# The last product of a gated MLP kernel: its second half of tokens first, to a bank of its own, combined and stored beside the first half

## The chip, the cores and the metric

One core of one Trainium2 chip. The metric is the device time of one execution in microseconds (us), of several executions, and beside it the span and the trace of one profiled execution.

## The reference

```python
# x: (8, 1024, 1024), w_gate and w_up: (1024, 4096), w_down: (4096, 1024), all float32
gate = x @ w_gate
up = x @ w_up
gate = 0.5 * gate * (1 + np.tanh(np.sqrt(2 / np.pi) * (gate + 0.044715 * gate ** 3)))
h = gate * up
return (h @ w_down).astype(np.float32)
```

## The kernel before

The 8192 tokens go through in eight passes of 1024. Each pass makes h for its tokens and multiplies it by w_down. From the fourth pass on both steps use a fast matrix scheme: fewer block products, more additions. The second step of such a pass is a list of 26 products of blocks. Their results are gathered in PSUM banks ("chains") and added by VectorE with signs into fp32 tiles; each of the 16 tiles is stored when it is complete. The list ends like this:

```python
DOWN = [
    # ... (cut)
    ('mul', 22, 'h5', 6, False),        # product into chain 6
    ('acc', 11, 11, 1, 1, -1, 1), ('acc', 5, 5, 1, -1, 1, -1), ('x',), ('x',),
    ('mul', 23, 'h1', 4, False),        # the last product, into chain 4
    ('acc', 5, 5, 6, -1, 1, 5), ('acc', 7, 7, 6, 1, -1, 9), ('x',), ('acc', 8, 8, 4, 1, 1, 2),
]
```

Only `('acc', 8, 8, 4, ...)` needs the last product; the two before it read chain 6. A product is 32 matmuls, two halves of tokens (m) in turn at each of 16 steps (j), both halves in one bank of 512 columns:

```python
def product(e, js):
    _, entry, h, c, first = e
    lhs, rhs = place[h], q_chunk(entry)
    for j in js:
        for m in range(2):
            nc.tensor.matmul(
                ps_all[:, bank[c], m * MQ : (m + 1) * MQ],     # MQ = 256
                lhs[:, j, m * P : (m + 1) * P],
                rhs[:, j, :],
                start=(first and j == 0 and m == 0),
                stop=(j == NP - 1),
                skip_group_check=True,
            )

def store(tile, o):
    q, c = divmod(o, 4)
    r0 = p * TOK + q * MQ
    nc.sync.dma_start(
        out=out2[r0 : r0 + MQ, c * MQ : (c + 1) * MQ].rearrange("(m p) c -> p m c", p=P),
        in_=tmp[:, t[tile]].rearrange("p (m c) -> p m c", m=2),
    )

# for an 'acc':
    nc.vector.scalar_tensor_tensor(
        tmp[:, t[v]], ps_all[:, bank[c]], float(sc * OSC), tmp[:, t[w]],
        MUL, ADD if st > 0 else SUB,
    )
# ... (cut: a store is put on a list and issued after the next product, or at the end)
```

## Time and profile before

| | us |
|---|---|
| time, median of 3 runs | 2256.03 (2255.78 to 2256.38) |
| span of the profiled execution | 2253.6 |
| TensorE busy | 2245.6 |
| last matmul ends | 2249.31 |
| last store lands (its last semaphore update) | 2.88 later |
| last instruction ends | 1.42 after that |

How to read it: nearly the whole span is one row of matmuls. What this change can touch is the tail, from the end of the last matmul to the end of the span, 4.30 us. I split it at the landing of the last store, because before the landing it is work (combine, issue, movement of the data, and the stretch from the last data to the landing, 0.35 us here) and after it only the engines' closing steps. That last stretch before the landing I call the confirmation. The ends, landings and closing steps are timestamps of the trace, which has them to a nanosecond; the page's views round to 0.01 or 0.1 us.

### The profile page before, as it was taken

What the parts mean: (1) busy time and instruction counts of PE and PEld (TensorE: products, weight loads), DVE (VectorE), ACT (ScalarE), POOL (GpSimd) and SP (SyncE); (2) the same over time, 40 slices, a digit from 0 to 9 for tenths busy, and PEclk for the clock granted to TensorE, in tenths of its full rate; (3) what the DMA queues carried; (4) which work ended last, traced back from release to release, by engine and by line L of the source; (5) the groups of instructions that cost most, each with busy time, mean ns of one, the idle gap of its engine ahead of it and who ended that gap; (6) DMA issues with size and microseconds to landing.
All of it is one profiled execution on the core that took longest, in us unless ns stands there. A gap on an engine that the chain in (4) does not pass through costs nothing.

```text
span 2253.6 us, 42764 instructions
## 1 busy us (share of the span) xinstructions
PE 2245.6 (100%) x16616; PEld 1624.2 (72%) x16616; DVE 1565.1 (69%) x2187; ACT 955.4 (42%) x1863; POOL 674.6 (30%) x825
## 2 busy tenths in 40 slices
PE   9999999999999999999999999999999999999999
PEld 4444444444444445888888888888888888888888
DVE  6666458883588755877776677666786667866674
ACT  4443135651365622666125550356404653055520
POOL 1332013330133300555014540255403543044520
PEclk9999999999999999999999999999999999999999
DMA  9898969999999999999998999988998889998886
GB/s 243 164 210 215 289 180 243 258 270 291 243 229 249 281 304 352 332 343 366 302 337 276 320 309 310 324 267 328 314 322 314 283 310 317 322 309 276 285 292 225
DMA packets 309117, 642.46 MB, mean 285 GB/s; under 512 B 79088, under 2 KB 185328, under 8 KB 288368
## 3 DMA queue, kind: packets, MB, share of 16 engines
q1 hardware_dynamic: 254128, 566.57, 73.5%
q0 software_dynamic: 54784, 73.14, 19.5%
q8 instruction: 130, 2.13, 0.4%
q14 instruction: 75, 0.61, 0.1%
HBM read 574.36 MB, written 138.41 MB: 316 GB/s over the span
## 4 chain that ended last, share of the span: by engine, by line
PE 87%; DMA 2%; SPq 1%; DVE 0%; issue 0%; DVEq 0%
PE ps L857 40%; PE ps L1108 20%; PE ps L635 17%; PE ps L1000 10%; DMA wd_quads<-x_sums 1%; SPq L255 0%; DMA ring<-wd_ops 0%; DVE x_sums L278 0%; DVE h_a L932 0%; DVE tmp L1177 0%; SPq L496 0%; DVEq L278 0%; SPq L544 0%
## 5 line engine op out<-in xcount | busy, mean ns | idle before, releaser
L857 PEld LDWEIGHTS <-ring 128*128 128x128 f16 x8320 | 814.1, 98 | 94.4
L834 POOL TENSOR_TENSOR h_a<-tmp 128x256 f16<-128x256 f32 x640 | 468.0, 750 | 840.6 <-ACT tmp L822 833.5
L857 PE MATMUL ps<-x_sums,ring 128*128 128x256 f16 x5760 | 655.8, 273 | 0.0
L819 DVE TENSOR_TENSOR tmp<-tmp,ps 128x512 f32<-128x512 f32 x640 | 414.3, 683 | 147.1 <-PE ps L857 90.2
L635 PEld LDWEIGHTS <-ring 128*128 128x128 f16 x2632 | 257.4, 98 | 311.2 <-DVE ring L360 0.9
L804 ACT COPY tmp<-ps 128x512 f32<-128x512 f32 x520 | 304.2, 585 | 237.0 <-PE ps L857 163.3
L635 PE MATMUL ps<-x_sums,ring 128*128 128x512 f16 x1504 | 340.1, 379 | 0.2 <-DVE ring L360 0.2
L822 ACT ACTIVATE tmp<-tmp 128x256 f32<-128x256 f32 x640 | 263.7, 418 | 173.2 <-DVE tmp L817 79.5
L857 PE MATMUL ps<-x_b,ring 128*128 128x256 f16 x2560 | 305.6, 273 | 0.0
L817 DVE TENSOR_TENSOR tmp<-ps,tmp 128x512 f32<-128x512 f32 x240 | 165.4, 689 | 145.2 <-ACT tmp L804 99.8
L635 PE MATMUL ps<-x_b,ring 128*128 128x512 f16 x1128 | 259.1, 379 | 0.0
L661 POOL TENSOR_TENSOR h_a<-tmp 128x512 f16<-128x512 f32 x94 | 141.1, 1501 | 377.4 <-ACT tmp L659 265.3
L1108 PEld LDWEIGHTS <-h_a 128*128 128x128 f16 x2240 | 219.2, 98 | 25.3
L1000 PE MATMUL ps<-ring,h_a 128*128 128x512 f16 x1024 | 222.3, 379 | 0.6 <-DMA ring<-wd_ops 0.6
L1108 PE MATMUL ps<-ring,h_a 128*128 128x256 f16 x1920 | 216.1, 273 | 0.0
L1000 PEld LDWEIGHTS <-h_a 128*128 128x128 f16 x1152 | 112.6, 98 | 136.8 <-DMA ring<-wd_ops 1.1
L654 DVE TENSOR_TENSOR tmp<-ps,tmp 128x512 f32<-128x512 f32 x188 | 127.3, 685 | 108.0 <-ACT tmp L646 106.5
L1165 ACT ACTIVATE tmp<-ps 128x512 f32<-128x512 f32 x60 | 35.3, 597 | 362.6 <-PE ps L1108 274.6
L1177 DVE SCALAR_TENSOR_TENSOR tmp<-ps,tmp 128x512 f32<-128x512 f32 x120 | 81.1, 690 | 97.5 <-PE ps L1108 66.7
L360 DVE TENSOR_TENSOR ring<-ring 128x1024 f16<-128x1024 f16 x188 | 139.7, 757 | 11.7 <-DMA ring<-in_w_up_dram 7.5
L646 ACT COPY tmp<-ps 128x512 f32<-128x512 f32 x188 | 109.8, 586 | 77.8 <-PE ps L635 77.8
L1108 PE MATMUL ps<-ring,x_sums 128*128 128x256 f16 x1120 | 126.3, 273 | 0.0
(102 smaller groups left out, 1534.0 us busy)
## 6 DMA issues: line engine op xcount, KB each, us to landing
ring<-w_ops SPq DMA_DIRECT2D x480, 512.0 KB, 4.9
ring<-wd_quads SPq DMA_DIRECT2D x110, 1024.0 KB, 6.9
ring<-wd_ops SPq DMA_DIRECT2D x35, 1024.0 KB, 8.2
out_dram<-tmp SPq DMA_DIRECT2D x128, 256.0 KB, 6.6
w_ops<-h_s SPq DMA_DIRECT2D x128, 256.0 KB, 6.8
ring<-in_w_gate_dram POOLq DMA_DIRECT2D x23, 1024.0 KB, 10.6
ring<-in_w_up_dram POOLq DMA_DIRECT2D x23, 1024.0 KB, 17.9
wd_quads<-x_sums SPq DMA_DIRECT2D x131, 128.0 KB, 6.5
```

The costliest lines, as they stand in the source:

```text
L360: nc.vector.tensor_tensor(o, a, b, op)
L635: nc.tensor.matmul(ps(b, w), lhs[:, k], rhs[:, k, :], start=(first and k == 0), stop=(k == KH - 1), skip_group_check=True,)
L654: nc.vector.tensor_tensor(o, ps("b", w), o, ADD)
L661: nc.gpsimd.tensor_tensor(hq[TO[n]][:, i, :], tmp[:, t[n, 1]], tmp[:, t[n, 0]], MUL)
L804: nc.scalar.copy(tmp[:, t[o[1]]], ps_all[:, bank[o[2]]])
L817: nc.vector.tensor_tensor(d, b, a, SUB)
L819: nc.vector.tensor_tensor(d, a, b, ADD if o[4] == "add" else SUB)
L822: nc.scalar.activation(d, d, GELU, scale=GSC)
L834: nc.gpsimd.tensor_tensor(h, tmp[:, t[o[1]], MQ : 2 * MQ], g, MUL)
L857: nc.tensor.matmul(ps_all[:, bank[c], w * MQ : (w + 1) * MQ], lhs[:, w, k], rhs[:, k], start=(first and w == 0 and k == 0), stop=(k == KH ...
L1000: nc.tensor.matmul(ps_all[:, bank[b, g]], lhs[:, j, g * P : (g + 1) * P], dc[:, n, :], start=(first and j == 0), stop=(j == NP - 1), skip_ ...
L1108: nc.tensor.matmul(ps_all[:, bank[c], m * MQ : (m + 1) * MQ], lhs[:, j, m * P : (m + 1) * P], rhs[:, j, :], start=(first and j == 0 and m ...
```

## The change

Intent: let the part of the work that has to wait for the very last matmul be half as large. The second half of the tokens is multiplied first, into a free bank; while TensorE then works on the first half, VectorE combines the second half and its store goes out. Only a combine of 256 columns and a store of 128 KB are left behind the last matmul. The core of the diff:

```diff
+        def last_product(e, events):
+            _, entry, h, c, _ = e
+            (fin,) = [f for f in events if f[0] == "acc" and f[3] == c]
+            # ... (cut)
+            other = ps_free.popleft()
+            d, (b0, b1) = tmp[:, t[v]], (slice(0, MQ), slice(MQ, 2 * MQ))
+
+            def part(m, b):
+                for j in range(NP):
+                    nc.tensor.matmul(
+                        ps_all[:, b, m * MQ : (m + 1) * MQ],
+                        place[h][:, j, m * P : (m + 1) * P],
+                        q_chunk(entry)[:, j, :],
+                        start=(m == 1 and j == 0),
+                        # ... (cut)
+                    )
+
+            def sum_up(b, s, op):
+                nc.vector.scalar_tensor_tensor(
+                    d[:, s], ps_all[:, b, s], float(sc * OSC), d[:, s], MUL, op
+                )
+
+            def send(m):
+                nc.sync.dma_start(
+                    out=out2[r0 + m * P : r0 + (m + 1) * P, o % 4 * MQ : (o % 4 + 1) * MQ],
+                    in_=d[:, m * MQ : (m + 1) * MQ],
+                )
+
+            part(1, other)
+            sum_up(bank[c], b1, ADD if st > 0 else SUB)
+            # ... (cut: stores that are due, the combines of chain 6, their stores)
+            part(0, bank[c])
+            sum_up(other, b1, ADD)
+            send(1)
+            sum_up(bank[c], b0, ADD if st > 0 else SUB)
+            send(0)
 # ... (cut)
+            if e[0] == "mul" and p == NPASS - 1 and i == end:
+                last_product(e, DOWN[i + 1 :])
+                break
```

More of the change, by code (lines that the diff above doesn't have):

```diff
@@ L1115, in product @@
                     )
+        def last_product(e, events):
+            _, entry, h, c, _ = e
+            (fin,) = [f for f in events if f[0] == "acc" and f[3] == c]
+            _, v, w, _, sc, st, o = fin
+            assert v == w and o >= 0 and not [f for f in events if f[0] == "snap"]
+            other = ps_free.popleft()
+            d, (b0, b1) = tmp[:, t[v]], (slice(0, MQ), slice(MQ, 2 * MQ))
+            r0 = p * TOK + o // 4 * MQ
+            def part(m, b):
[5 more added lines that the diff above has]
+                        start=(m == 1 and j == 0),
+                        stop=(j == NP - 1),
+                        skip_group_check=True,
+                    )
[10 more added lines that the diff above has]
+            sum_up(bank[c], b1, ADD if st > 0 else SUB)
+            for f in todo:
+                f()
+            todo.clear()
+            for f in events:
+                if f[0] == "acc" and f is not fin:
+                    acc(f)
+            for f in todo:
+                f()
+            todo.clear()
+            part(0, bank[c])
[3 more added lines that the diff above has]
+            send(0)
@@ new lines, in acc, with last @@
+        def acc(e):
+            _, v, w, c, sc, st, o = e
+            if v not in t:
+                t[v] = tmp_free.popleft()
+            nc.vector.scalar_tensor_tensor(
+                tmp[:, t[v]], ps_all[:, bank[c]], float(sc * OSC), tmp[:, t[w]],
+                MUL, ADD if st > 0 else SUB,
+            )
+            if v != w:
+                used(w, DOWN.index(e))
+            if o >= 0:
+                def last(v=v, o=o):
+                    store(v, o)
+                    tmp_free.append(t.pop(v))
+                todo.append(last)
+            if last_chain[c] == DOWN.index(e):
+                ps_free.append(bank[c])
@@ L1139, in down_fast @@
         count = 0
+        end = max(i for i, e in enumerate(DOWN) if e[0] == "mul")
         for i, e in enumerate(DOWN):
+            if e[0] == "mul" and p == NPASS - 1 and i == end:
+                last_product(e, DOWN[i + 1 :])
+                break
             if e[0] == "mul":
@@ L1173, in down_fast @@
             elif e[0] == "acc":
-                _, v, w, c, sc, st, o = e
-                if v not in t:
-                    t[v] = tmp_free.popleft()
-                nc.vector.scalar_tensor_tensor(
-                    tmp[:, t[v]], ps_all[:, bank[c]], float(sc * OSC), tmp[:, t[w]],
-                    MUL, ADD if st > 0 else SUB,
-                )
-                if v != w:
-                    used(w, i)
-                if o >= 0:
-                    def last(v=v, o=o):
-                        store(v, o)
-                        tmp_free.append(t.pop(v))
-                    todo.append(last)
-                if last_chain[c] == i:
-                    ps_free.append(bank[c])
+                acc(e)
             elif work:
```

## The prediction

> **What bounds the kernel now.** I read the page's busy shares first, then the slices, then the chain that ended last, and only then the last 10 us. The busy shares:
>
> ```profile
> span 2253.6 us, 42764 instructions
> ...
> PE 2245.6 (100%) x16616; PEld 1624.2 (72%) x16616; DVE 1565.1 (69%) x2187; ACT 955.4 (42%) x1863; POOL 674.6 (30%) x825
> ```
>
> TensorE is busy for the whole span but for 8.0 us; no other engine is near. The slices show full granted clock throughout. The change leaves the number and kind of matmuls as they are, so it can win only in those 8 us, and of them only in the part at the end. The chain of waits in order of time shows how little that is (start, length, what):
>
> ```profile
> 1976.84 181.65 PE ps L857 x1664
> 2158.49 90.84 PE ps L1108 x832
> 2249.33 0.02 issue
> 2249.35 0.69 DVE tmp L1177
> ```
>
> From 279 us on the chain is TensorE alone: the five last passes are blocks of 181.65 to 181.69 and of 90.83 or 90.84 us, so repeatable to 0.04 us. 90.84/832 = 109.2 ns from matmul to matmul, and 181.65/1664 = 109.2 ns in the block before. Behind the last matmul hangs one VectorE instruction. The timeline of the last 8 us (start, length, engine, line, what, idle before it and its releaser):
>
> ```profile
> 2245.33 3.98 PE L1108 MATMUL ps<-ring,h_a 128*128 128x256 f16 x35
> ...
> 2245.86 1.29 DVE L1177 SCALAR_TENSOR_TENSOR tmp<-ps,tmp 128x512 f32<-128x512 f32 x2 [2.15 <-PE ps L1108]
> 2246.58 3.87 SPq L1120 DMA_DIRECT2D out_dram<-tmp  x3
> 2249.35 0.69 DVE L1177 SCALAR_TENSOR_TENSOR tmp<-ps,tmp 128x512 f32<-128x512 f32 x1 [2.20 <-PE ps L1108]
> ```
>
> The two combines at 2245.86 start when the last product but one is done. The last product is 32 matmuls, 32 x 109.2 ns = 3.49 us, so from about 2245.83 to 2249.33. Two stores go out beside it; the third waits for the last combine. Only that store, 256 KB, is then left. I cut this rest into four stretches (from:to, us, busy time by engine PE, PEld, DVE, ACT, POOL, granted clock, DMA share, GB/s):
>
> ```profile
> 2250.07:2250.98 0.91, 0.00 (x0) 0.00 (x0) 0.00 (x0) 0.00 (x0) 0.00 (x0) 1.00 0.02 7
> 2250.98:2251.76 0.78, 0.00 (x0) 0.00 (x0) 0.00 (x0) 0.00 (x0) 0.00 (x0) 1.00 0.95 323
> 2251.76:2252.36 0.60, 0.00 (x0) 0.00 (x0) 0.00 (x0) 0.00 (x0) 0.00 (x0) 1.00 0.03 7
> 2252.36:2253.60 1.24, 0.00 (x0) 0.00 (x0) 0.00 (x0) 0.00 (x0) 0.00 (x0) 0.78 0.02 7
> ```
>
> First the store is issued[...] (0.91 us from the start of the issue to the first data), then the data moves (0.78 us)[...], then the engines' closing barrier (1.24). The store's row gives the same from the other side:
>
> ```profile
> L1120 SPq DMA_DIRECT2D out_dram<-tmp x1: 372/372/372, 2250.1 to 2250.1; - x1
> ...
> DMA to landing us min/median/max: 2.1/2.1/2.1
> ```
>
> So the tail after the last matmul is 2253.60 - 2249.33 = 4.27 us, 0.19% of the span. That is the most that any change of it could give, and a change of 2% would have to be 45 us.
>
> [...]this trace has 690 for the same combine[...]. No fp32 row with 256 columns is here, but fp16 additions of 128x512[...] take 416 to 424[...]. [...]the rate is 0.26 MB in 0.78 us, some 340 GB/s; [...]
>
> **The change, part by part.**
> *Matmuls.* 32 before, 32 after, the same weights and moving data. Only the order changes: before, the halves alternate at each step; after, 16 into columns 256 to 511 of another bank, then 16 into columns 0 to 255 of the old one. Consecutive matmuls now accumulate into the same columns. The 181.65 us block does that already (groups of four into one half), at 109.2 ns. Cost 0; the last matmul stays at 2249.33.
> *The other bank.* I walked the list of products with its queue of free banks: before the last product six are free, and the one at the head was given back many products earlier. In the instruction order of both builds the first matmul of the new part waits only for the weights' transfer. Cost 0.
> *VectorE.* One 512-wide combine becomes three 256-wide ones. (a) The sum so far of the old bank, second half, has no wait of its own and stands behind the combines of the product two before, which end at 2243.71: it runs at 2243.71 to 2244.13, where VectorE idles 2.15 us. (b) The new bank's half is complete after 16 x 109.2 ns = 1.75 us of the last product, at 2247.58; the two older combines end at 2245.86 + 1.29 = 2247.15, so it runs 2247.62 to 2248.04. (c) The first half, behind the last matmul: 2249.35 to 2249.77. Only (c) is on the path: 0.690 - 0.424 = 0.27 us gained.
> *TensorE's new wait.* The first weights of the second half now wait for VectorE: that is (a), read before the bank's other columns are written. It is done 3.4 us earlier. Cost 0.
> *Stores.* 256 KB become two of 128 KB. The first is issued at about 2248.08, behind the older two (issues end by 2247.6), and lands about 1.7 us later, at 2249.8, before the last store moves a byte. The last is issued at 2249.77 + 0.03 = 2249.80. Its pattern is plain rows; such issues here take 319 ns at the least, against 372: 0.05 us gained. 128 rows of 1 KB instead of 256 in the same queues: 0.78/2 = 0.39 us gained. Start, confirmation and closing barrier stay.
> *Sum.* 0.27 + 0.05 + 0.39 = 0.71 us. The tail goes from 4.27 to 3.56 us, the span from 2253.60 to 2252.89, and the time from 2256.03 to 2255.3.
>
> **The rivals.**
> *The store's fixed part takes it all.* If the 0.78 us were not bytes but the arrival of descriptors, the last store would take 2.1 us as before and only 0.27 to 0.3 us would be left: 2255.7. Against it: DMA share 0.95 at 323 GB/s, the rate at which the two older stores moved back to back.
> *The extra store is in the way.* One more issue (0.37 us) and 128 KB could push the last one back, if the first were late. It is issued 1.7 us before the last; for a collision (b) would have to be 0.9 us later than I have it. It would give back up to 0.4 us: 2255.7.
> *The new wait stalls TensorE.* If the weights of the second half waited not for (a) but for the older two combines, these still end at 2247.15, 0.4 us ahead of need. If they waited for (b), TensorE would stand for 0.46 us[...]. But (b) comes after those matmuls in program order, so they can't wait for it.
> *Accumulating 16 times running into the same columns is slower.* Each extra 10 ns per matmul would cost 0.32 us. The older block's equal cadence with runs of four speaks against it.
> *Nothing can be seen.* The three runs before span 0.60 us (2255.78 to 2256.38), and the profiled run had 2255.39. The variation comes from the first 279 us, where the chain has transfers of 8.5 to 9.7 us in it. The gain is about as large as this spread, so medians of three may show 0.3 or 1.1 us.
>
> **Range and chances.** The centre is 2255.3. The mechanism could be 0.4 us worse, hardly more than 0.2 better; a median of three wanders by about 0.3. Together 2254.6 to 2256.0 for 8 in 10. Faster by 2% is impossible with a tail of 0.19%[...]. Chances: 0.005 faster, 0.99 within 2%, 0.005 slower.
>
> **What would show each step.** In the profile after: the last block of the chain still about 90.84 us long; three combines visible: one of 128x256 near 2243.7, one near 2247.6, one behind the last matmul, each of 0.42 us; two stores of 128 KB, the last landing after about 1.7 us instead of 2.1; DMA busy for 0.39 us at the very end; the barrier of 1.24 us unchanged. I'm wrong if the last matmuls show a gap in the middle of the last product, if the last store still lands after 2.1 us, or if the time differs by over 1 us from 2255.3, which would point to something outside the tail.

The sum came to 0.27 + 0.05 + 0.39 = 0.71 us. Of the first term I had worked out the 0.424 us of a combine of 256 columns. What the trace of the kernel before gives for it is an estimate: the combine of 512 fp32 columns takes 690 ns there, about as long as an addition of 1024 fp16 columns (684 ns for the 25 of `x_sums<-x_b,x_sums`; other names have means of up to 929), so one of 256 should take about what an addition of 512 fp16 columns takes, 416 to 424 ns in the rows that the prediction names. That start, confirmation and closing stay as they are was an assumption, and so was that the half that goes first needs a bank of its own. The third of the four stretches, 0.60 us there, is the confirmation.

## The result, and the profile after

| | before | after |
|---|---|---|
| median of 6 runs, us | 2255.91 (2254.71 to 2256.97) | 2255.2 (2254.26 to 2255.86) |
| span of the profiled execution, us | 2253.6 | 2252.9 |
| last matmul ends, us | 2249.31 | 2249.60 |
| from there to the landing of the last store, us | 2.88 | 2.35 |
| from the landing to the end, us | 1.42 | 0.94 |

The ratio of the times is 0.9996, with a 95% interval of 0.9984 to 1.0009. A ratio here is the mean time of one kernel's runs over that of the other's of the same rounds, so not quite the ratio of the medians in the table. The interval holds 1, and single runs of one kernel differ by up to 2.3 us in these rounds. So the times alone don't show a gain; the tail in the trace does.

The busy shares after are as good as equal:

```profile
span 2252.9 us, 42769 instructions
...
PE 2245.2 (100%) x16616; PEld 1624.1 (72%) x16616; DVE 1560.6 (69%) x2189; ACT 956.4 (42%) x1863; POOL 680.6 (30%) x825
```

The chain of waits after (start, length, what):

```profile
2158.77 87.33 PE ps L1108 x800
2246.10 3.51 PE ps L1130 x32
2249.61 0.02 issue
2249.64 0.42 DVE tmp L1140
```

The last block is split over two lines of the program now, and 87.33 + 3.51 = 90.84 us is to the last digit what one line had before. So 16 matmuls in a row into the same columns, the change of bank and TensorE's new wait on VectorE cost nothing. What hangs behind is a 0.42 us combine instead of one of 0.69.

But the last block starts at 2158.77 instead of 2158.49, so 0.28 us later. That comes from the first 279 us, as the same chain of both kernels shows where TensorE's long row begins, before:

```profile
278.93 27.80 PE ps L1000 x128
```

and after:

```profile
279.21 27.80 PE ps L1000 x128
```

VectorE in the timeline of the last 10 us after:

```profile
2242.70 1.29 DVE L1171 SCALAR_TENSOR_TENSOR tmp<-ps,tmp 128x512 f32<-128x512 f32 x2 [2.86 <-PE ps L1108]
2243.91 0.41 DVE L1140 SCALAR_TENSOR_TENSOR tmp<-ps,tmp 128x256 f32<-128x256 f32 x1
2246.14 1.29 DVE L1171 SCALAR_TENSOR_TENSOR tmp<-ps,tmp 128x512 f32<-128x512 f32 x2 [1.82 <-PE ps L1108]
2247.89 0.42 DVE L1140 SCALAR_TENSOR_TENSOR tmp<-ps,tmp 128x256 f32<-128x256 f32 x1 [0.46 <-PE ps L1130]
2249.64 0.42 DVE L1140 SCALAR_TENSOR_TENSOR tmp<-ps,tmp 128x256 f32<-128x256 f32 x1 [1.32 <-PE ps L1130]
```

The three small combines stand where the prediction put them: one in an idle stretch, one in the middle of the last product, and one behind it. The last store, from its issue to the end, in four stretches (the columns as in the prediction's fence of the same kind):

```profile
2250.09:2250.93 0.84, 0.00 (x0) 0.00 (x0) 0.00 (x0) 0.00 (x0) 0.00 (x0) 1.00 0.00 1
2250.93:2251.44 0.51, 0.00 (x0) 0.00 (x0) 0.00 (x0) 0.00 (x0) 0.00 (x0) 1.00 0.75 255
2251.44:2251.95 0.51, 0.00 (x0) 0.00 (x0) 0.00 (x0) 0.00 (x0) 0.00 (x0) 1.00 0.00 0
2251.95:2252.89 0.94, 0.00 (x0) 0.00 (x0) 0.00 (x0) 0.00 (x0) 0.00 (x0) 0.51 0.03 9
```

Start 0.84, movement 0.51, confirmation 0.51, closing 0.94 us. (The clock column is under 1 only in the last stretch: 0.51 here, 0.78 in the prediction's fence.) The landing is 0.53 us earlier against the last matmul, and the closing is 0.48 us shorter than before, which the prediction did not have. The closing shows in the sync engine's own rows (count, then shortest, median and longest in ns). Before, one DRAIN of three took 130 ns (DRAIN is one of the instructions of the closing; here only its time matters):

```profile
L1346 SPq DRAIN  x3: 7/7/130, 2252.4 to 2253.1; - x3
```

After, none did:

```profile
L1403 SPq DRAIN  x3: 7/7/7, 2252.1 to 2252.4; - x3
```

In the trace's timestamps the slow DRAIN before begins 348 ns after the one ahead of it; after the change that distance is 65 ns. So the tail became 1.01 us shorter (4.30 to 3.29), of which 0.28 us was taken back by the later start of the row of matmuls, a part that the change doesn't touch: 0.73 us of span.

### The profile page after: what moved, and what is told of

It reads as the page before. It is cut to its first block, busy times and chain, and to the rows that moved or that the text cites. A ratio compares the mean times of both kernels' runs of the same rounds, so it can differ in the third digit from the quotient of the medians.

```text
span 2252.9 us, 42769 instructions
## 1 busy us (share of the span) xinstructions
PE 2245.2 (100%) x16616; PEld 1624.1 (72%) x16616; DVE 1560.6 (69%) x2189; ACT 956.4 (42%) x1863; POOL 680.6 (30%) x825
## 3 DMA queue, kind: packets, MB, share of 16 engines
q8 instruction: 130, 2.13, 0.4%
## 4 chain that ended last, share of the span: by engine, by line
PE 87%; DMA 2%; SPq 1%; DVE 0%; issue 0%; DVEq 0%
PE ps L857 40%; PE ps L1108 20%; PE ps L635 17%; PE ps L1000 10%; DMA wd_quads<-x_sums 1%; SPq L255 0%; DMA ring<-wd_ops 0%; PE ps L1130 0%; DVE x_sums L278 0%; DVE h_a L932 0%; DVE tmp L1140 0%; SPq L496 0%; DVEq L278 0%; SPq L544 0%
```

## The experiments

Two questions were left. Do both parts, combine and store, pay as computed, and is the bank needed? And is the shorter closing chance, a result of the smaller last store, or something else? Since the times can't resolve half a microsecond, the verdicts rest on the tail in each run's trace. "Sync instr." is the number of instructions that the trace lists for the sync engine.

| run | last matmul to landing | landing to end | tail | sync instr. | time, median | before, same rounds |
|---|---|---|---|---|---|---|
| before, first profile | 2.88 | 1.42 | 4.30 | 2387 | | |
| after, first profile | 2.35 | 0.94 | 3.29 | 2389 | 2255.2 | 2255.91 |
| before again | 2.89 | 1.42 | 4.31 | 2387 | 2255.7 (1 run) | 2255.17 |
| one store | 2.61 | 1.42 | 4.03 | 2387 | 2254.55 | 2255.17 |
| split behind | 2.85 | 0.90 | 3.75 | 2390 | 2254.26 | 2255.17 |
| store moved in the program | 2.35 | 0.93 | 3.28 | 2389 | 2254.72 | 2255.17 |
| before plus one | 2.89 | 1.34 | 4.23 | 2388 | 2255.81 | 2255.39 |
| first store by ScalarE | 2.36 | 1.32 | 3.67 | 2387 | 2254.38 | 2255.39 |
| held back | 2.77 | 1.33 | 4.11 | 2388 | 2256.16 | 2255.39 |
| quarters | 2.28 | 1.72 | 4.00 | 2390 | 2255.28 | 2255.39 |
| before plus two | 2.91 | 0.94 | 3.85 | 2389 | 2255.4 | 2255.26 |
| change again | 2.35 | 0.93 | 3.28 | 2389 | 2254.0 | 2255.26 |

(All in us but the count. All results were correct. Every ratio to the kernel before that was taken lay between 0.9996 and 1.0002, each with an interval that holds 1.)

In these twelve profiles the last matmul ended between 2248.62 and 2250.86 us. This spread of 2.2 us is twice the whole effect, and the change has no part in it. The long row of matmuls starts between 278.24 and 279.56 us. From its first matmul to the last one nine profiles take 1970.37 to 1970.39 us, before and after alike; in the other three (store moved in the program, before plus one, quarters) TensorE waits again between 413 and 494 us, which adds 0.4, 0.9 and 2.2 us.

### The kernel before, again

No edit.

> The kernel before, unchanged, once more. In its first profile the last store landed 2.88 us after the last matmul, and the span ended 1.42 us after that landing, with one of the sync engine's closing DRAINs at 130 ns and a gap of 0.35 us ahead of it; in the changed kernel these were 2.35 and 0.94 us, and no such DRAIN. Theory A (the closing stall is chance or belongs to the build, not to the change's idea): matmul to landing again 2.88 within 0.05, landing to end anywhere from 0.94 to 1.42. If it is chance it may well be 0.94 here. Rival B (the old ending always has the stall): landing to end again 1.42. The start of the long TensorE chain was 278.93 before and 279.2 after: if the first 279 us only vary by chance, it will differ from 278.93 by some tenths here too.

Both parts of the tail came within 0.01 us of the first profile, the slow DRAIN too:

```profile
L1346 SPq DRAIN  x3: 7/7/130, 2252.7 to 2253.4; - x3
```

So the stall is no chance of one execution. Only the start varied: the last matmul ended 0.30 us later than in the first profile.

### The VectorE part alone: one store

```diff
             sum_up(other, b1, ADD)
-            send(1)
             sum_up(bank[c], b0, ADD if st > 0 else SUB)
-            send(0)
+            store(v, o)
```

> The VectorE part of the change alone: other bank and early combine of the second half, but both halves leave in one store of 256 KB behind the last combine. Theory A (both parts pay): last combine 0.42 us as in the changed kernel, store as before (2.13 us from issue to last landing), so last matmul to landing 2.88 - 0.27 = 2.62 us. Rival C (only the store's size matters): 2.88. Rival D (the combine alone gives all of it): 2.35. Time within 0.2 per cent of before, so only the profile can tell.

2.61 us, as theory A had it: the shorter combine alone gives 0.27 us, neither nothing nor all. The timeline shows the combine and the store that follows it at once:

```profile
2249.87 0.42 DVE L1140 SCALAR_TENSOR_TENSOR tmp<-ps,tmp 128x256 f32<-128x256 f32 x1 [1.32 <-PE ps L1130]
...
2250.32 0.37 SPq L1188 DMA_DIRECT2D out_dram<-tmp  x1
```

The closing was long again, 1.42 us.

### The splitting alone, behind the last matmul

```diff
-            part(1, other)
-            sum_up(bank[c], b1, ADD if st > 0 else SUB)
+            ps_free.append(other)
+            product(e, range(NP))
             # ... (cut: the combines of chain 6 and their stores, as they were)
-            part(0, bank[c])
-            sum_up(other, b1, ADD)
+            sum_up(bank[c], b1, ADD if st > 0 else SUB)
             send(1)
             sum_up(bank[c], b0, ADD if st > 0 else SUB)
             send(0)
```

> The splitting alone, without another bank and without a new order of the matmuls: the product as before, then two combines of 256 columns each and two stores of 128 KB, all behind the last matmul. Theory A: combines end 0.46 and about 0.86 us after the last matmul, stores issued at 0.49 and 0.89, the last one's data follows the first one's, landing 0.89 + 1.86 = 2.75 us after the last matmul: 0.13 better than before, 0.40 worse than the change, so that the bank and the order do most of the work. Rival E (pipelining of combine and store is enough, no bank needed): 2.35 to 2.45. Rival F (a second store close behind the first waits for it): 2.9 or more.

2.85 us: 0.03 better than before and 0.10 worse than I expected. Without the bank and the new order the halves don't pay: the second combine and the second issue queue up behind the first ones, as the timeline shows.

```profile
2248.65 0.76 DVE L1140 SCALAR_TENSOR_TENSOR tmp<-ps,tmp 128x256 f32<-128x256 f32 x2 [2.21 <-PE ps L1108]
...
2249.11 0.82 SPq L1145 DMA_DIRECT2D out_dram<-tmp  x2
```

This run takes away the bank and the order together. No run has the new order with both halves in one bank, so whether a bank of its own is needed is not shown here.

Its tail is nevertheless 0.55 us shorter than before, 0.52 of it by the closing, which is the short one here. That spoke against "it is chance", and for something that goes with the additional store.

### An attempt to hold the first store back that did not

```diff
             sum_up(other, b1, ADD)
-            send(1)
             sum_up(bank[c], b0, ADD if st > 0 else SUB)
+            send(1)
             send(0)
```

> The change as it is, but the store of the second half is held back and issued just ahead of the last one. Theory A (the first store must be early, because each issue holds the queue for 0.34 us): last issue at 0.49 + 0.40 = 0.9 us after the last matmul, data of the two back to back, landing at about 2.75 us instead of 2.35. Rival G (issues overlap with the movement, nothing lost): 2.35 to 2.5. Closing part from landing to end 0.9 to 1.4.

My expectation missed because the edit does nothing: in this program a store waits for the combine that it needs, not for the combine that stands ahead of it, and the sync engine's own order stayed the same. The first store was issued 1.26 us ahead of the last matmul's end, exactly as in the change. As a repeat of the change it is of use: 2.35 and 0.93 us again.

### Before plus one sync instruction

In the kernel before, the store ahead of the last, which is hidden beside the last product, leaves in two halves:

```diff
             r0 = p * TOK + q * MQ
+            if p == NPASS - 1 and o == 9:
+                for m in range(2):
+                    nc.sync.dma_start(
+                        out=out2[r0 + m * P : r0 + (m + 1) * P, c * MQ : (c + 1) * MQ],
+                        in_=tmp[:, t[tile], m * MQ : (m + 1) * MQ],
+                    )
+                return
```

> The kernel before with nothing of the change but its one extra instruction on the sync engine: the store ahead of the last (hidden beside the last product) leaves in two halves. So far the closing part, from the last landing to the end, was 1.42 us in three profiles of kernels with the old count of stores (before twice, one store) and 0.90 to 0.94 in three with one store more (the change, split behind, the change with its first store moved in the program). Theory B2 (the position of the closing instructions in the sync engine's stream decides; one instruction more is enough): last matmul to landing 2.88 as before, landing to end 0.90 to 0.94, tail 3.8 instead of 4.3. Rival H (the closing is shorter because the last store is small): landing to end 1.42, tail 4.30.

Theory B2 in this form fell: the closing was 1.34, not 0.93. But the stall had moved. It was not at the second DRAIN but at the first, one instruction earlier (in the timestamps: the first DRAIN begins 364 ns after the wait ahead of it and takes 131 ns). The row alone, from the view of the closing line, still shows one slow DRAIN:

```profile
L1353 SPq DRAIN  x3: 7/7/131, 2253.1 to 2253.5; - x3
```

The stall is at the 2384th instruction that the trace lists for the sync engine in every profile that has one, whatever instruction that is. The kernel before lists 2387, this one 2388, the change 2389: its first store needs an issue and a separate wait. In the change the 2384th is the wait for the last store itself.

The timestamps of the kept traces show that this place is one of a row. At listed instruction 80 and at every 128th after it, up to the 2384th, the sync engine begins 336 ns or more after the end of the instruction ahead, in all 19 places of all twelve profiles (median 343 to 347 ns). No other place in the round of 128 has a gap of over 56 ns each time. And within 4.8 us of each of the 19 places a DMA transfer of 8192 bytes of the kind "instruction" begins; only some 15% of all moments are followed by one so soon. At the 2384th it begins 0.97 to 1.26 us after the instruction ahead has ended, in all twelve profiles, also in those whose closing is short. So the stall seems to be there every time, and what the count decides is whether it falls behind the landing or is hidden by a wait.

### The change with its first store issued by ScalarE

```diff
-            def send(m):
-                nc.sync.dma_start(
+            def send(m, queue=nc.sync):
+                queue.dma_start(
 # ...
-            send(1)
+            send(1, nc.scalar)
```

> The whole change, but its first store is issued by ScalarE, so that the sync engine has the old count of instructions again. Theory B2: last matmul to landing 2.35 as in the change, but landing to end 1.42 again, tail 3.77: what came by the extra instruction is lost. Rival H: tail 3.29 as in the change.

The sync engine is back at 2387 instructions, and the stall is back at the second DRAIN, with the small last store and everything else of the change in place:

```profile
L1403 SPq DRAIN  x3: 7/7/130, 2251.3 to 2252.0; - x3
```

So rival H, that a small last store shortens the closing, is out. The closing is 1.32 and not 1.42, because of a second, smaller thing: the stores take eight completion semaphores in turn, and the closing waits for them in a fixed order. Before, the last store has the seventh, so one more wait comes behind it, in this comparison worth 0.10 us. With one store more it has the eighth, and no wait is left.

### The first store really held back

```diff
             sum_up(other, b1, ADD)
-            send(1)
             sum_up(bank[c], b0, ADD if st > 0 else SUB)
             send(0)
+            send(1)
```

> The change with the two stores swapped in the sync engine's queue, so that the second half's store really goes out last, behind the first half's (the earlier attempt to hold it back changed the program's order and not the queue's). Theory A: issues at 0.49 and about 0.88 us after the last matmul, landing at about 2.83 as with the splitting behind (2.85), closing 0.9: tail 3.75, 0.46 worse than the change. Rival G: 2.35 to 2.5.

Now the queue's order is changed, and the landing is at 2.77 instead of 2.35 us (2.83 expected): 0.42 us lost. So rival G is out: that the first store goes out early is a necessary part. The closing was 1.33, not 0.9. The held back store needs no wait of its own, so there are 2388 instructions and the stall is at the first DRAIN, as in "before plus one".

### One step further: quarters

```diff
-            sum_up(bank[c], b0, ADD if st > 0 else SUB)
-            send(0)
+            for q, queue in ((0, nc.sync), (1, nc.scalar)):
+                s = slice(q * P, (q + 1) * P)
+                sum_up(bank[c], s, ADD if st > 0 else SUB)
+                queue.dma_start(
+                    out=out2[r0 : r0 + P, o % 4 * MQ + q * P : o % 4 * MQ + (q + 1) * P],
+                    in_=d[:, s],
+                )
```

> One step further: the first half's combine and store in two quarters of 128 columns, the first quarter's store by the sync engine, the second's by ScalarE's queue. VectorE: about 0.29 us for 128 columns, the second follows about 0.25 later, so issues at 0.36 and 0.61 us after the last matmul; the last data then ends at about 1.7 instead of 1.85. Theory A carried on: landing 2.20 to 2.30, closing 0.9 (the sync engine's count is that of the change), tail 3.1 to 3.25. Against it: [...]2.4 or more.

(Its 0.29 us is an estimate that the traces of before and after also give: 0.692 us for 512 columns and 0.425 for 256, so 0.27 less for 256 fewer and 0.13 less for another 128. The two quarters took 0.49 us together.)

The landing is 0.07 us earlier (2.28), as expected, but the closing takes 1.72 us, which I had not expected. The store added takes the next semaphore in turn, which stands near the front of the closing's order. So eight waits, one after the other, come after the landing instead of one. The 2384th instruction is one of them: it begins 0.36 us after the one ahead of it, where its neighbours follow in 0.06 to 0.09. So of the 0.79 us that the closing is longer than in the change, some 0.29 is the stall and the rest, 0.5 us, the seven waits more. The step loses 0.7 us of tail against the change.

### Before plus two sync instructions

As "before plus one", and the combine of that hidden store is done in two halves too, so that the second half's store needs a wait of its own:

```diff
+                halves = p == NPASS - 1 and o == 9
+                for s in (slice(0, MQ), slice(MQ, 2 * MQ)) if halves else (slice(0, 2 * MQ),):
                     nc.vector.scalar_tensor_tensor(
-                        tmp[:, t[v]], ps_all[:, bank[c]], float(sc * OSC), tmp[:, t[w]],
+                        tmp[:, t[v], s], ps_all[:, bank[c], s], float(sc * OSC), tmp[:, t[w], s],
# ... (cut: the rest of the call, and the edit of "before plus one")
```

> In all profiles with a long closing the stall sits at the same place of the sync engine's stream: the 2384th instruction that the trace lists for it, whatever stands there (2387 listed in all: its second DRAIN; 2388: its first). The changed kernel has 2389, and there the 2384th is the wait for the last store itself. Theory B3 (a place in the stream costs some 0.3 to 0.4 us, and the wait for the landing hides it if it falls there or earlier): the kernel before with two more instructions, by a combine ahead of the last (hidden beside the last product) done in two halves, each with its own store: last matmul to landing 2.88 as before, landing to end 0.93 as in the change, tail 3.8 instead of 4.3. Rival H (the closing is short only where the last store is small): 1.3 to 1.4, tail 4.3. Time about 0.5 us under before, within the spread of single runs.

2.91, 0.94 and 3.85 us. No DRAIN is slow:

```profile
L1355 SPq DRAIN  x3: 7/7/7, 2252.4 to 2252.7; - x3
```

and the last work is what it was in the kernel before:

```profile
2249.43 0.69 DVE L1186 SCALAR_TENSOR_TENSOR tmp<-ps,tmp 128x512 f32<-128x512 f32 x1 [2.14 <-PE ps L1108]
...
2250.15 0.38 SPq L1127 DMA_DIRECT2D out_dram<-tmp  x1
```

So the old kernel, with its big last combine and its big last store, gets the short closing from two more instructions in the sync engine's stream. Theory B3 holds. Its time did not show it (2255.4 against 2255.26): 0.45 us is below what five runs resolve.

### The change, again

No edit.

> The changed kernel once more, with more rounds, on a chip of its own call: last matmul to landing 2.35, landing to end 0.93, tail 3.29, each within 0.05. The first 279 us decide the rest: start of the long TensorE chain within 1 us of 279.2. Time 0.5 to 1.2 us under before if the rounds average the first part out; a sign that is not clear is as likely, as single runs of one kernel differ by 1 to 2 us.

2.35, 0.93 and 3.28 us. The median is 2254.0 against 2255.26, ratio 0.9996, interval 0.9984 to 1.0009. The sign is again that of a gain and again not clear of the noise.

## Why the prediction was right

The time (2255.2, predicted 2255.3) lies in the range and the class is right. The mechanism was right as well, but the agreement to 0.1 us is luck: one term was too large, one was missing, the start of the row of matmuls shifted, and each median is of six runs that spread over 1.6 to 2.3 us.

- *Matmuls and the other bank, cost 0.* Right: 90.84 us before and after, and no gap.
- *VectorE, 0.27.* Right: 0.692 to 0.425 us, against the estimate of 424 ns, and with the store left whole the landing moved by just 0.27 us. (The fp16 additions that speak for the 424 are picked rows: others of the same shape in that trace have means of 439 to 482 ns.) The two early combines came within 0.1 us of the predicted places, once the 0.28 us shift is taken off.
- *The new wait, cost 0.* Right: the read that TensorE waits for ended at 2244.32, and the second part of the product began 3.36 us later, with a matmul at 2247.69 that follows the one ahead of it without a gap.
- *The first store out of the way.* Right in what matters. Its landing took 2.0 us, not 1.7, but came 0.57 us before the last store moved its first byte. Held back, it costs 0.42 us.
- *The last store, 0.05 + 0.39.* The failing step is "Start, confirmation and closing barrier stay". The start was 0.05 us shorter (0.89 to 0.84, from the issue to the first data) and the movement 0.38 us shorter (0.89 to 0.52 from the first byte to the last), as predicted. But the confirmation, from the last data to the last landing, grew from 0.35 to 0.51 us. From issue to landing 256 KB took 2.13 us and 128 KB 1.86, so the gain was 0.27 and not 0.44. The issue's own row went from 372 to 345 ns, 0.03 and not 0.05. The prediction had also cut the four stretches a little off: by the timestamps they are 0.89, 0.89, 0.35 and 1.42 us before, where it has 0.91, 0.78, 0.60 and 1.24, since the last store landed at 2252.20 and not at 2252.36. Over all runs the big last store took 0.35 to 0.37, the small one of the first half 0.50 to 0.51, that of the second half (held back) and the quarter 0.43. What sets it was not found; size and place in memory changed together in these runs.
- *The closing, unchanged.* Wrong, by the same step: it was 0.48 us shorter. About 0.4 of this (0.38 to 0.41 by three comparisons) is the stall at a place in the sync engine's stream, hidden by the wait for the landing as soon as two more instructions stand ahead of it; the rest, 0.07 to 0.10, is one semaphore wait less. The first is shown by taking it away in the kernel before and by bringing it back in the change. The stall cost about 0.4 us in six of the twelve profiles and 0.29 in a seventh, always at the 2384th listed instruction. What the stall is, is not shown: it comes every 128 listed instructions, and a transfer of 8192 bytes of the kind "instruction" follows within 4.8 us each time, but no run changed either (and the trace may not list every instruction).
- *Sum.* Predicted 0.71: 0.27 + 0.44. Measured in the tail 1.01: 0.27 + 0.27 + 0.48, less roundings.
- *"Nothing can be seen".* This rival came true for the times: both sets of rounds, of six and five, give 0.9996 with an interval that holds 1. The tail, repeated in three profiles of the change to 0.01 us, is what shows the gain. The prediction put the variation into the first 279 us; three of the twelve profiles have more of it, between 413 and 494 us.

Of its idea the change gives 0.53 us, 0.02% of the time. The rest, 0.48 us, belongs to the count of sync instructions and to the turn of the last store's semaphore and could be had without it; the version "before plus two" has it (its tail is 0.45 us shorter). No version here beats the change: of all twelve tails its 3.28 to 3.29 us are the shortest.

## What to carry to other kernels

Halving what hangs behind the last matmul paid here only with the first half out of the way: combined beside the matmuls, for which this change uses a bank of its own, and its store issued well ahead of the last one (1.75 us in the change). With both the landing came 0.53 us earlier, with the halves behind the last matmul 0.03, with the first store held back 0.11. When an effect is a thousandth of the time or less, measure it where it arises, from one fixed event to the next in the trace, and repeat the profile; the total is blurred by parts that the change doesn't touch (here the last matmul ended anywhere within 2.2 us). And when a term that should not move does, count instructions and look at what stands where before giving the change the credit.
